# Value products of prompt attention: one head's values in two parts as the stationary operand, two passes and a sum

## The chip, the cores and the metric

One core of one Trainium2 chip runs the whole program. The metric is the device time of one execution in microseconds (us). The profile was taken of a single execution on that core; times of instructions are in us unless ns is written.

## What is computed

One inference step of a layer with two groups of attention heads side by side, then a gated feed-forward part, for 512 prompt tokens and 8 x 16 sampled tokens (640 tokens together, model width 2048). One input projection gives queries, keys and values of group A (16 heads of width 64, a frame sees its own chunk of 64 and the eight before it) and of group B (16 query heads over 2 key and value heads, window of 128, sinks, partial rotary). The core of a head is

```python
p = jnp.exp(s - m)
denom = jnp.sum(p, axis=-1, keepdims=True)
w = (p / denom).astype(v.dtype)
o = jnp.einsum('bghrqk,bgkhd->bgqhrd', w, v)
...
o = jnp.concatenate([rmsnorm(oa, norm_grp_a), rmsnorm(ob, norm_grp_b)], axis=-1)
x = x + o @ w_out
h = rmsnorm(x, norm_ffn)
return x + (jax.nn.silu(h @ w_gate) * (h @ w_up)) @ w_down
```

The change concerns the `einsum` of `w` and `v` for the prompt tokens, in both groups.

## The kernel before, in words

Everything is held with features (or keys) in the 128 partitions and tokens along the free axis. The matmuls take their operands as float32r; to keep float32 accuracy each operand is split into a rounded part `hi` and a rest `lo` (`split`, lines 137 to 139: ACT writes `hi`, DVE subtracts to give `lo`), and each product takes three passes, `hi*hi + hi*lo + lo*hi` (`mm3`, lines 145 to 149). So line 147, 148 and 149 are the first, second and third pass of every product in the program, and lines 138 and 139 are the two halves of every split.

The order of work. `dense` (line 159) computes one 128-row tile of an output for all 640 tokens: for each block of 8 feature tiles it splits the weights (two slots each for `hi` and `lo` and two blocks at a time, so the next block's split can begin when the block before the present one is done with), then issues 6 matmuls of 320 columns for each feature tile. After each of these groups of 6 it calls `pump` (line 72), which emits one more stage of the side work. Side work is attention, written as generators: each `yield` ends a stage. Two streams of heads run beside the projections; from p = 4 on (line 660) one of the two streams is given to the sampled tokens ("decode"), so that the prompt heads of group A have the other alone. The framework then orders the instructions of each engine itself from these emissions, within the dependences; each engine works through its own list in order.

Slots. On-chip tiles are handed out in order of return from lists ("S": 128 x 640 floats, "W": 128 x 1024 floats). `n.bank()` takes one of four PSUM banks ("at") for side work; the projections have two pairs of their own ("dn").

A head of group A (`prompt_a`, line 354): scores of four query tiles with a mask and a maximum on DVE, exponentials on ACT, division on DVE, then `flip` (line 341): transposes of the 128 x 128 blocks into a bank, split into `hi` and `lo`. The value product follows (lines 376 to 384): with `v` of 128 key rows by 128 columns as the stationary operand, `p` moves through in pieces of 512, 384, 128 and 256 columns, three passes each, all into one bank `ps`. The 128 columns of `v` are the values of two heads, 64 each, but a head needs only its own 64 rows of the output; `tensor_copy` (line 387) takes these rows to the tile `ot`. When both heads of a pair are done, `ot` is written to `oa_d` in DRAM, which the output projection reads back much later (line 680).

A head of group B (`prompt_b`, line 390) does the same with pieces of 256, 256, 256 and 128 columns (lines 412 to 416) and the copy of line 419; here the 128 columns of `vb` are the two value heads.

The values themselves are made in `values` (line 448): transposes of the projected tile into a bank, then one split of 128 x 512 into `hi` and `lo`; for group B also the 128 sampled tokens, of which `decode_b` uses `cut(vb, SP, TOK)` (line 506).

Of the kernel before, what the change touches and what calls it, by code (L numbers as in the profile page):

```python
# [13 lines left out]
P = 128  # L14
D = 2048
KT = 16
TOK = 640
# [14 lines left out]


def active(step):
    """Pairs of ff tiles on chip in a step of the second half: each stays for eight steps."""
    return [j for j in range(NPAIR) if (step - START[j]) % STEPS < 8]


# [9 lines left out]


class Net:  # L50
    """Emission helpers over a fixed set of on-chip slots handed out in program order."""

    def __init__(self, nc, tc, io, pools):
        self.nc, self.tc, self.io, self.pools = nc, tc, io, pools
# [15 lines left out]
        self.queues.setdefault(queue, []).append(work)  # L70

    def pump(self):
        """Emit one more stage of the side work; streams take turns."""
        for _ in range(len(self.streams)):
            name, queue = self.streams[self.turn % len(self.streams)]
            self.turn += 1
            work = self.active.get(name)
            if work is None and self.queues.get(queue):
                work = self.active[name] = self.queues[queue].pop(0)
            if work is None or work.gi_running:  # L80
                continue
            try:
                next(work)
            except StopIteration:
                self.active[name] = None
            return True
        return False
# [21 lines left out]
        self.lists.setdefault(lst, []).extend(self.owner.pop(id(t))[0] for t in tiles)  # L109

    def keep_turns(self):
        """A slot's tiles take it in program order."""
        first = {}
        for block in self.nc.cur_f.blocks:
            for ins in block.instructions:
                for o in ins.outs or ():
                    ap = getattr(o, "bass_ap", None)
                    if ap is not None:
                        first.setdefault(ap.tensor.name, ins)
        info = mybir.DependencyInfo(mybir.DependencyClass.NoSync, mybir.DependencyReason.DATA)  # L120
        for names in self.turns.values():
            for x, y in zip(names, names[1:]):
                self.tc.add_manual_dep(first[y], first[x].name, info, reason="slot order")
# [21 lines left out]
    def mm3(self, out, a, b, first, last):  # L145
# [2 lines left out]
        mm(out, a[0], b[1], start=False, stop=False)  # L148
        mm(out, a[1], b[0], start=False, stop=last)  # L149

    def weights(self, src, kt, lst="WH"):
        raw, hi, lo = self.get("WR"), self.get(lst), self.get(lst)
        self.nc.sync.dma_start(out=sh(raw, kt, P), in_=src)
        w = [r(sh(hi, kt, P)), r(sh(lo, kt, P))]
        self.split(sh(raw, kt, P), *w)
        self.put("WR", raw)
        return kt, w, (lst, hi, lo)

    def dense(self, chunks, acts, outs=1):
        """One tile of outputs, or several that share the passes over acts."""  # L160
        ps = [self.banks() for _ in range(outs)]
        k = 0
        for i in range(0, len(chunks), outs):
            now = [c if len(c) == 3 else self.weights(*c) for c in chunks[i:i + outs]]
            for j in range(now[0][0]):
                ah, al = acts[k]
                for (_, w, _), out in zip(now, ps):
                    for a in range(2):
                        t = slice(a * HT, a * HT + HT)
                        self.mm3(out[:, a], (w[0][:, j], w[1][:, j]), (ah[:, t], al[:, t]), k == 0, k == len(acts) - 1)  # L170
                    self.pump()
                k += 1
            for _, _, own in now:
                self.put(*own)
        return ps if outs > 1 else ps[0]

    def rstd_steps(self, parts, dim, out):
        """1 / sqrt(mean + eps) of the tokens of each half, in all partitions."""
        nc = self.nc
        ps, n = self.bank(), len(parts)  # L180
        blocks = (0, P, HT - P)
# [43 lines left out]
def r(ap):  # L225
    return ap.bitcast(F32R)


def build(nc, tc, io, pools):
# [31 lines left out]
    oa_d, ob_d = dram("oa_d", (8, P, TOK)), dram("ob_d", (8, P, TOK))  # L261
    sa_d, sb_d = dram("sa_d", (3, P, 8, P)), dram("sb_d", (P, 8, P))

# [1 line left out]
    n.move("S", "C", 7)  # L265
    n.move("S", "F", 3)
    n.move("W", "WR", 2)
    n.move("W", "WH", 4)
    r_mix, cos, sin, kb0, kb1, vb0, vb1 = (n.get("C") for _ in range(7))
    kb, vb = (r(kb0), r(kb1)), (r(vb0), r(vb1))  # L270

# [1 line left out]
    START_CHUNKS = {0: (24, 0, 2, "S"), 1: (25, 0, 2, "S"), 2: (24, 2, 8, "WH"), 4: (25, 2, 8, "WH"),  # L273
                    8: (24, 8, 16, "W"), 10: (25, 8, 16, "W")}
    xg, acts, xs = [], [], []
# [38 lines left out]
        nc.vector.tensor_tensor(halves(out), ps, halves(r_mix), ALU.mult)  # L314
        return out

# [1 line left out]
    def scores(q, k, rr, i, k0, k1, bias, s, mx):  # L318
        ps = n.bank()[:, :k1 - k0]
        rows = slice(64 * rr, 64 * rr + 64)  # L320
# [33 lines left out]
    def prompt_a(h, q, k, v, ot, done):  # L354
# [19 lines left out]
        o1, p13 = flip([blk(i, 1) for i in range(1, 4)] + [blk(3, 3)], "S")  # L374
        yield
        ps = n.bank()
        n.mm3(ps, cut(v, 0, 128), p0, True, False)
        n.put("S", *o0)
        o2, p2 = flip([blk(i, 2) for i in range(2, 4)], "S")
        n.put("S", t0, t1)  # L380
        yield
        n.mm3(ps[:, 128:], cut(v, 128, 256), cut(p13, 0, 384), False, False)
        n.mm3(ps[:, 384:], cut(v, 384, 512), cut(p13, 384, 512), False, False)
        n.mm3(ps[:, 256:], cut(v, 256, 384), p2, False, True)
        n.put("S", *o1, *o2)
        rows = slice(64 * rr, 64 * rr + 64)
        nc.vector.tensor_copy(ot[rows, :SP], ps[rows])
        done()

    def prompt_b(t, rr, q, ot, done):  # L390
        sink = sinks[:, 8 * rr + t:8 * rr + t + 1]
        t0, t1 = n.get("S"), n.get("S")
        es = [t0[:, 512:640], t0[:, :256], t0[:, 256:512], t1[:, :256]]
        mx = n.small(4)
        for pick in ((0, 1), (2, 3)):
            for i in pick:
                k0 = max(0, i - 1) * P
                w = (i + 1) * P - k0
                scores(q, kb, rr, i, k0, k0 + w, mask_b[:, 256 - w:], es[i], mx[:, i:i + 1])
            yield  # L400
        softmax(es, mx, sink)
        yield
        yield
        yield
        yield
        oa, pa = flip([es[0], es[1][:, :P], es[2][:, P:], es[3][:, :P]], "S")
        yield
        ob, pb = flip([es[1][:, P:], es[2][:, :P], es[3][:, P:]], "S")
        n.put("S", t0, t1)
        yield  # L410
        ps = n.bank()
        n.mm3(ps[:, 0:256], cut(vb, 0, 128), cut(pa, 0, 256), True, False)
        n.mm3(ps[:, 256:512], cut(vb, 256, 384), cut(pa, 256, 512), False, False)
        yield
        n.mm3(ps[:, 128:384], cut(vb, 128, 256), cut(pb, 0, 256), False, False)
        n.mm3(ps[:, 384:512], cut(vb, 384, 512), cut(pb, 256, 384), False, True)
        n.put("S", *oa, *ob)
        rows = slice(64 * rr, 64 * rr + 64)
        nc.vector.tensor_copy(ot[rows, :SP], ps[rows])
        done()  # L420

    def heads_of(kind, p, held, *args):
# [22 lines left out]
        nc.vector.tensor_tensor(x[:80], x[:80], rot[:80], ALU.add)  # L445
        n.put("S", rot)

    def values(vf, hi, lo, cols):
        for c in range(0, cols, 512):
            w = min(512, cols - c)  # L450
            ps = n.bank()[:, :w]
            for j in range(w // P):
                tr(ps[:, j * P:(j + 1) * P], vf[:, c + j * P:c + (j + 1) * P])
            n.split(ps, hi[:, c:c + w], lo[:, c:c + w])

    def decode_b():
        os_b = n.get("W")
        o_s = sh(os_b, 8, P)
        for hf in range(2):
# [17 lines left out]
            for bb in range(4):  # L477
# [25 lines left out]
                yield  # L503
                po = n.bank()[:, :256]
                n.mm3(po, (vd[0][:, bb], vd[1][:, bb]), cut(pt2, 0, 256), True, False)
                n.mm3(po, cut(vb, SP, TOK), cut(pt2, 256, 512), False, True)
                n.put("S", *own)
                for j in range(2):
                    rows = slice(64 * j, 64 * j + 64)
# [95 lines left out]
        dma(out=oa_d[4 * g:4 * g + 4, :, SP:].rearrange("t p c -> p t c"), in_=sh(o_s, 4, P))  # L605
        n.put("D", o_s, bias, *z, *held)

# [1 line left out]
    n.add("heads", input_norm())  # L609
    ps_k, ps_v = n.dense(first, acts, 2)  # L610
    n.drain()
# [4 lines left out]
    n.put("F", kf)  # L616
    vf = proj(25, ps_v)
    dma(out=io["o_vb"], in_=vf)
    values(vf, *vb, TOK)
    n.put("F", vf)  # L620

    def project_b(t):
# [9 lines left out]
    def project_a(p):  # L632
# [16 lines left out]
        dma(out=sa_d[2, :, p], in_=vf[:, SP:])  # L649
        vo = n.get("W")  # L650
        v = pack(vo, SP)
        values(vf, *v, SP)
        n.put("F", vf)
        heads_of(prompt_a, p, [("W", x) for x in (ko, qo, vo)], q, k, v)

# [13 lines left out]
            n.add("decode", decode_a(0))  # L669
        project_a(p)  # L670

# [1 line left out]
    n.put("S", *xg, r_mix)  # L673
    n.move("F", "S", 3)

# [33 lines left out]
    n.put("S", r_b, *own_b)  # L709
    n.move("D", "S", 10)  # L710

# [1 line left out]
    more = group_operands(oa_d, g_a, ssq_a, range(4, 8))  # L713
    own_a, acts_a = own_a + more[0], acts_a + more[1]

    def prepare(kts, in_place=()):
        """The seven left operands of pairs of feature tiles, one product at a time."""
        work = []
        for kt in kts:
            scale = lambda t, m: nc.scalar.activation(t[:, :TOK], x2[m], AF.Identity, scale=g_ffn[:, m:m + 1])  # L720
# [45 lines left out]
                pass  # L766
    n.put("S", r_a, ssq_a, *own_a)

# [1 line left out]
    n.move("WH", "H", 4)  # L770
    n.move("WR", "W1", 2)
    n.lists["W"] = n.lists.pop("W1") + n.lists["W"]

    def quartet(k, load, lefts, before=None, after=None, part="all"):
        """Weights b11, b12, b21, b22 against the seven left operands; yields each
        product's name and bank. The late part has the two products that only add
        to the first half of the tokens."""

        def product(src, which, bank):
            own = n.get("H"), n.get("H")  # L780
# [126 lines left out]
                n.put("S", *gate, *y)  # L907
    n.put("S", r_f)

# [1 line left out]
    sums, waiting = [], []  # L911

    def fetch_waiting(left):
# [59 lines left out]
            for i in range(2):  # L973
                n.add_square(ssq, sums[t % 8][i], t == STEPS - 8 and i == 0, "S")

# [1 line left out]
    r_y = n.get("S")  # L977

    def squares(q, half):
# [129 lines left out]
```

## Time and profile before

| what | value |
|---|---|
| runs of the kernel (us) | 2723.32, 2725.25, 2726.64; median 2725.25 |
| span of the profiled execution, first to last instruction | 2722.2 us |
| its mean granted TensorE clock | 0.988 |
| instructions in the profile | 45156 |
| largest groups of PE | lines 147, 148 and 149, 3694 matmuls of 320 columns each into "dn" |

The page gives the profiled execution no time other than its span, which is 3.05 us below the median of the runs; sums made from its rows are set against 2722.2 us and carried over to 2725.25 us as a difference.

How to read it: a row of a timeline gives the start, the duration, the engine, the line and the operation. PE is TensorE's matmuls, PEld its loads of the stationary operand, which run beside the matmuls. A matmul's duration includes its way through the array and overlaps the next one, so what a matmul costs is the distance from its start to the start of the next. "idle before, releaser" names what an engine last waited for. The granted clock is a share of full speed. Tile names have their numbers left out: "at" is a side-work bank, "dn" a projection bank, "S", "W" and "C" slots.

### The profile page before, as it was taken

Reading aid. Unit: us, or ns where it says so; the run is one execution under the profiler, and the core shown is the slowest. Engines: PE = TensorE matmul, PEld = TensorE weight load, DVE = VectorE, ACT = ScalarE, POOL = GpSimd, SP = SyncE. Lnnn points to the kernel's source line nnn. Section 1 sums busy time; section 2 is a strip of 40 time slices with the busy share of each in tenths; the row PEclk is TensorE's granted clock in tenths of the full one; section 3 lists DMA queues with packets and bytes.
Section 4 is the critical chain, followed back from the end, with each engine's and each line's share of the span. In section 5 each row is a group of like instructions: output and inputs, shape, how many; then the busy total and the mean of one; then the engine's idle time right before and its main releaser. Section 6 shows DMA issues by size and latency. Waiting matters only on the chain.

```text
span 2722.2 us, 45156 instructions
## 1 busy us (share of the span) xinstructions
PE 2645.7 (97%) x17757; PEld 2584.7 (95%) x17757; DVE 1933.8 (71%) x2947; ACT 1063.8 (39%) x1718; POOL 787.2 (29%) x564
## 2 busy tenths in 40 slices
PE   7999999999999999999999999999999899999986
PEld 7999999899899999999999999999999899999986
DVE  6555565655666678776767667667677878888897
ACT  4333333433544454333333333333334444444443
POOL 3000000000212123333343333333434533444453
PEclk9999999999899999999999999999999999999998
DMA  5222223333556443333232333332334644444334
GB/s 163 86 77 76 82 75 100 108 117 113 165 182 214 148 141 109 103 105 124 96 119 103 111 116 106 108 119 101 120 103 152 228 130 130 134 127 133 109 115 134
DMA packets 154149, 332.25 MB, mean 122 GB/s; under 512 B 18065, under 2 KB 69265, under 8 KB 153937
## 3 DMA queue, kind: packets, MB, share of 16 engines
q1 hardware_dynamic: 153936, 329.38, 36.9%
q8 instruction: 139, 2.28, 0.3%
q14 instruction: 74, 0.60, 0.1%
HBM read 274.38 MB, written 54.20 MB: 121 GB/s over the span
## 4 chain that ended last, share of the span: by engine, by line
PE 60%; DVE 5%; DMA 3%; issue 2%; ACT 1%; POOL 1%; SPq 0%; DVEq 0%; POOLq 0%; ACTq 0%
PE dn L149 12%; PE dn L147 12%; PE dn L148 12%; PE at L149 8%; PE at L148 8%; PE at L147 8%; DVE W L139 2%; DMA S<-act_d 1%; DVE S L828 1%; DMA W<-w_down 1%; DVE S L999 0%; DVE S L139 0%; DVE W L809 0%; DVE S L841 0%; POOL S L212 0%
## 5 line engine op out<-in xcount | busy, mean ns | idle before, releaser
L147 PE MATMUL dn<-S,W 128*128 128x320 f32 x3694 | 1164.8, 315 | 16.4 <-DVE S L828 6.3
L149 PE MATMUL dn<-S,W 128*128 128x320 f32 x3694 | 1150.5, 311 | 16.4 <-DVE W L139 16.4
L148 PE MATMUL dn<-S,W 128*128 128x320 f32 x3694 | 1148.9, 311 | 2.2 <-DVE S L143 1.1
L138 ACT ACTIVATE W<-W 128x1024 fp32r<-128x1024 f32 (+2 forms) x632 | 609.4, 965 | 1085.3 <-PE dn L148 551.4
L139 DVE TENSOR_TENSOR W<-W,W 128x1024 fp32r<-128x1024 f32 (+2 forms) x632 | 770.1, 1219 | 134.8 <-ACT W L138 130.2
L147 PEld LDWEIGHTS dn<-S,W 128*128 128x128 f32 x3694 | 699.5, 189 | 35.1 <-issue 17.3
L149 PEld LDWEIGHTS dn<-S,W 128*128 128x128 f32 x3694 | 699.4, 189 | 21.3 <-DVE W L139 21.0
L148 PEld LDWEIGHTS dn<-S,W 128*128 128x128 f32 x3694 | 700.0, 190 | 4.0 <-DVE S L143 1.4
L149 PE MATMUL at<-S,W 128*128 128x320 f32 (+2 forms) x1658 | 514.3, 310 | 7.5 <-DVE W L139 7.4
L147 PE MATMUL at<-S,W 128*128 128x320 f32 (+2 forms) x1658 | 513.6, 310 | 1.1 <-ACT W L138 1.1
L148 PE MATMUL at<-S,W 128*128 128x320 f32 (+2 forms) x1658 | 513.3, 310 | 0.2 <-DVE S L139 0.2
L811 POOL TENSOR_TENSOR W<-W,W 128x1024 f32<-128x1024 f32 (+2 forms) x76 | 162.8, 2142 | 587.0 <-DVE W L139 450.6
L149 PEld LDWEIGHTS at<-S,W 128*128 128x128 f32 x1658 | 311.3, 188 | 11.0 <-DVE W L139 10.3
L147 PEld LDWEIGHTS at<-S,W 128*128 128x128 f32 x1658 | 311.4, 188 | 1.6 <-ACT W L138 1.4
L148 PEld LDWEIGHTS at<-S,W 128*128 128x128 f32 x1658 | 311.3, 188 | 0.5 <-DVE S L139 0.5
L828 DVE TENSOR_TENSOR S<-S,dn 128x320 f32<-128x320 f32 x358 | 164.2, 482 | 104.0 <-PE dn L149 102.7
L807 DVE TENSOR_TENSOR W<-W,W 128x1024 f32<-128x1024 f32 (+2 forms) x76 | 140.2, 1845 | 89.4 <-DMA W<-w_up 46.6
L818 POOL TENSOR_TENSOR W<-W,W 128x1024 f32<-128x1024 f32 (+2 forms) x76 | 166.7, 2193 | 112.5 <-DVE W L139 107.0
L828 DVE TENSOR_TENSOR S<-S,at 128x320 f32<-128x320 f32 x262 | 123.5, 481 | 71.0 <-PE at L149 71.0
L212 POOL TENSOR_TENSOR S<-S,S 128x640 f32<-128x640 f32 x40 | 75.3, 1882 | 161.8 <-ACT S L211 161.4
L809 DVE TENSOR_TENSOR W<-W,W 128x1024 f32<-128x1024 f32 (+2 forms) x76 | 82.9, 1090 | 31.8 <-DMA W<-w_gate 23.0
L139 DVE TENSOR_TENSOR S<-at,S 128x512 fp32r<-128x512 f32 (+2 forms) x108 | 64.0, 604 | 53.0 <-ACT S L138 52.2
(141 smaller groups left out, 2306.6 us busy)
## 6 DMA issues: line engine op xcount, KB each, us to landing
W<-w_gate SPq DMA_DIRECT2D x88, 512.0 KB
W<-w_up SPq DMA_DIRECT2D x88, 512.0 KB
W<-w_in SPq DMA_DIRECT2D x66, 512.0 KB
W<-w_down SPq DMA_DIRECT2D x64, 384.0 KB
W<-w_down SPq DMA_DIRECT2D x68, 320.0 KB
act_d<-S SPq DMA_DIRECT2D x66, 320.0 KB
half<-act_d SPq DMA_DIRECT2D x81, 160.0 KB
S<-act_d SPq DMA_DIRECT2D x80, 160.0 KB
```

The source lines that it names most:

```text
L138: self.nc.scalar.activation(hi, src, AF.Identity)
L139: self.nc.vector.tensor_tensor(lo, src, f(hi), ALU.subtract)
L147: mm(out, a[0], b[0], start=first, stop=False)
L148: mm(out, a[0], b[1], start=False, stop=False)
L149: mm(out, a[1], b[0], start=False, stop=last)
L212: (eng or nc.gpsimd).tensor_tensor(ssq, ssq, sq, ALU.add)
L807: nc.vector.tensor_tensor(b12[:, w], b12[:, w], b22[:, w], sub)
L809: nc.vector.tensor_tensor(s6[:, w], b11[:, w], b12[:, w], sub)
L811: nc.gpsimd.tensor_tensor(b11[:, w], b22[:, w], s6[:, w], sub)
L818: nc.gpsimd.tensor_tensor(b21[:, w], b21[:, w], s6[:, w], sub)
L828: add = lambda o, a, b: nc.vector.tensor_tensor(o, a, b, ALU.add)
```

## The change

A second helper takes two passes with one stationary operand. The tile with one head's values now holds `hi` and `lo` side by side, 64 columns each, for each block of 128 keys, so the passes give `hi*p` in output rows 0 to 63 and `lo*p` in rows 64 to 127, with `p` being `hi` and then `lo` of the weights. A new `both` moves the lower half of the bank by ACT into an "S" slot and adds the upper half to it on DVE. `values` makes one such tile for each of two heads with two splits of half the size; the own values of the sampled tokens in group B get a tile view of their own (`vb_own`). Comments and docstrings are removed too.

```diff
+    def mm2(self, out, a, b, first, last):
+        mm = self.nc.tensor.matmul
+        mm(out, a, b[0], start=first, stop=False)
+        mm(out, a, b[1], start=False, stop=last)
...
-    kb, vb = (r(kb0), r(kb1)), (r(vb0), r(vb1))
+    kb = (r(kb0), r(kb1))
+    vb_own = tuple(r(x[:, SP:]) for x in (vb0, vb1))
...
         ps = n.bank()
-        n.mm3(ps, cut(v, 0, 128), p0, True, False)
+        vr = v[rr]
+        n.mm2(ps, vr[:, 0:128], p0, True, False)
...
-        n.mm3(ps[:, 128:], cut(v, 128, 256), cut(p13, 0, 384), False, False)
-        n.mm3(ps[:, 384:], cut(v, 384, 512), cut(p13, 384, 512), False, False)
-        n.mm3(ps[:, 256:], cut(v, 256, 384), p2, False, True)
+        n.mm2(ps[:, 128:], vr[:, 128:256], cut(p13, 0, 384), False, False)
+        n.mm2(ps[:, 384:], vr[:, 384:512], cut(p13, 384, 512), False, False)
+        n.mm2(ps[:, 256:], vr[:, 256:384], p2, False, True)
         n.put("S", *o1, *o2)
-        rows = slice(64 * rr, 64 * rr + 64)
-        nc.vector.tensor_copy(ot[rows, :SP], ps[rows])
+        both(ot, rr, ps)
         done()
...
-        n.mm3(ps[:, 0:256], cut(vb, 0, 128), cut(pa, 0, 256), True, False)
-        n.mm3(ps[:, 256:512], cut(vb, 256, 384), cut(pa, 256, 512), False, False)
-        yield
-        n.mm3(ps[:, 128:384], cut(vb, 128, 256), cut(pb, 0, 256), False, False)
-        n.mm3(ps[:, 384:512], cut(vb, 384, 512), cut(pb, 256, 384), False, True)
+        vr = r((vb0, vb1)[rr])
+        n.mm2(ps[:, 0:256], vr[:, 0:128], cut(pa, 0, 256), True, False)
+        n.mm2(ps[:, 256:512], vr[:, 256:384], cut(pa, 256, 512), False, False)
+        yield
+        n.mm2(ps[:, 128:384], vr[:, 128:256], cut(pb, 0, 256), False, False)
+        n.mm2(ps[:, 384:512], vr[:, 384:512], cut(pb, 256, 384), False, True)
         n.put("S", *oa, *ob)
-        rows = slice(64 * rr, 64 * rr + 64)
-        nc.vector.tensor_copy(ot[rows, :SP], ps[rows])
+        both(ot, rr, ps)
         done()
...
-    def values(vf, hi, lo, cols):
-        for c in range(0, cols, 512):
-            w = min(512, cols - c)
-            ps = n.bank()[:, :w]
-            for j in range(w // P):
-                tr(ps[:, j * P:(j + 1) * P], vf[:, c + j * P:c + (j + 1) * P])
-            n.split(ps, hi[:, c:c + w], lo[:, c:c + w])
+    def values(vf, sides):
+        ps = n.bank()
+        for j in range(4):
+            tr(ps[:, j * P:(j + 1) * P], vf[:, j * P:(j + 1) * P])
+        for rr, v in enumerate(sides):
+            src = ps.rearrange("p (j c) -> p j c", j=4)[:, :, 64 * rr:64 * rr + 64]
+            v = v.rearrange("p (j c) -> p j c", j=4)
+            n.split(src, v[:, :, :64], v[:, :, 64:])
+
+    def both(ot, rr, ps):
+        t = n.get("S")
+        nc.scalar.activation(t[:64, :SP], ps[64:], AF.Identity)
+        nc.vector.tensor_tensor(ot[64 * rr:64 * rr + 64, :SP], t[:64, :SP], ps[:64], ALU.add)
+        n.put("S", t)
...
-                n.mm3(po, cut(vb, SP, TOK), cut(pt2, 256, 512), False, True)
+                n.mm3(po, vb_own, cut(pt2, 256, 512), False, True)
...
-    values(vf, *vb, TOK)
+    values(vf, [r(x[:, :SP]) for x in (vb0, vb1)])
+    ps = n.bank()[:, :P]
+    tr(ps, vf[:, SP:])
+    n.split(ps, *vb_own)
...
-        values(vf, *v, SP)
+        values(vf, v)
```

## Rows read from the trace of the kernel before

**Rows 1.** The page: span, and busy time of each engine.

```profile
span 2722.2 us, 45156 instructions
...
PE 2645.7 (97%) x17757; PEld 2584.7 (95%) x17757; DVE 1933.8 (71%) x2947; ACT 1063.8 (39%) x1718; POOL 787.2 (29%) x564
```

**Rows 2.** Busy time by stage: stretch, length, PE, PEld, DVE, ACT, POOL (instructions), clock, DMA.

```profile
57.00:440.00 383.00, 382.45 (x2618) 364.71 (x2618) 217.12 (x518) 129.31 (x307) 5.35 (x12) 1.00 0.24 81
440.00:770.00 330.00, 326.65 (x2141) 303.05 (x2140) 212.91 (x549) 144.02 (x324) 33.53 (x82) 0.98 0.38 126
```

**Rows 3.** Timeline, PE, one A head's value product: start, us, engine line operation.

```profile
169.88 0.39 PE L149 MATMUL at<-S,W 128*128 128x512 f32 x1
...
170.11 0.38 PE L248 MATMUL at<-cst,S 128*128 128x128 f32 x2
...
171.56 0.35 PE L149 MATMUL at<-S,W 128*128 128x384 f32 x1
...
171.74 0.22 PE L147 MATMUL at<-S,W 128*128 128x128 f32 x1
...
171.91 0.27 PE L149 MATMUL at<-S,W 128*128 128x128 f32 x1
...
172.03 0.33 PE L147 MATMUL at<-S,W 128*128 128x256 f32 x1
...
172.31 0.28 PE L149 MATMUL at<-S,W 128*128 128x256 f32 x1
...
172.43 0.31 PE L147 MATMUL dn<-S,W 128*128 128x320 f32 x1
```

**Rows 4.** Groups by shape, 57 to 770 us, PE: counts of the third passes.

```profile
L149 PE MATMUL at<-S,S 128*128 128x256 f32 x64 | 18.0, 283 | 0.0
...
L149 PE MATMUL at<-S,W 128*128 128x512 f32 x16 | 6.3, 394 | 0.0
...
L149 PE MATMUL at<-S,S 128*128 128x128 f32 x16 | 4.4, 273 | 0.0
```

**Rows 5.** Groups by shape, 57 to 770 us, ACT and DVE reading a bank, with their waits.

```profile
L139 DVE TENSOR_TENSOR S<-at,S 128x512 fp32r<-128x512 f32 x59 | 40.0, 688 | 39.9 <-ACT S L138 39.5
...
L138 ACT ACTIVATE S<-at 128x512 fp32r<-128x512 f32 x59 | 34.8, 593 | 63.8 <-PE at L248 61.5 <-DMA S<-S 2.1
...
L419 DVE COPY S<-at 64x512 f32<-64x512 f32 x16 | 11.0, 687 | 16.0 <-PE at L149 16.0
...
L387 DVE COPY S<-at 64x512 f32<-64x512 f32 x16 | 11.0, 687 | 3.7 <-PE at L149 3.5
...
L139 DVE TENSOR_TENSOR S<-at,S 128x256 fp32r<-128x256 f32 x16 | 6.7, 420 | 7.1 <-ACT S L138 7.1
...
L138 ACT ACTIVATE S<-at 128x256 fp32r<-128x256 f32 x16 | 6.1, 380 | 19.5 <-PE at L248 10.9 <-DVE S L445 8.6
```

**Rows 6.** Timeline: weight splits on ACT and DVE in a stretch without attention.

```profile
70.97 1.06 ACT L138 ACTIVATE W<-W 128x1024 fp32r<-128x1024 f32 x1 [5.35 <-issue]
...
72.06 1.23 DVE L139 TENSOR_TENSOR W<-W,W 128x1024 fp32r<-128x1024 f32 x1 [0.17 <-ACT W L138]
...
77.96 1.06 ACT L138 ACTIVATE W<-W 128x1024 fp32r<-128x1024 f32 x1 [5.93 <-PE dn L148]
```

**Rows 7.** Line 387's copies by stage: stretch, length, DVE (instructions), clock, DMA share, GB/s.

```profile
440.00:770.00 330.00, 6.85 (x10) 0.98 0.38 126
```

**Rows 8.** Busy time in short stretches, columns as rows 2.

```profile
710.00:715.00 5.00, 4.14 (x30) 3.78 (x29) 3.25 (x7) 4.28 (x6) 3.35 (x6) 1.00 0.60 204
715.00:720.00 5.00, 5.00 (x20) 3.83 (x19) 3.42 (x8) 4.16 (x7) 1.99 (x2) 0.55 0.54 167
720.00:725.00 5.00, 5.00 (x20) 4.56 (x19) 3.91 (x8) 1.12 (x2) 2.70 (x3) 0.50 0.61 204
```

**Rows 9.** Tile oa_d, its writes and reads: durations in ns, first and last start.

```profile
L429 SPq DMA_DIRECT2D oa_d<-S x8: 326/327/327, 175.9 to 768.6; - x8
L680 SPq DMA_DIRECT2D S<-oa_d x8: 320/323/434, 829.5 to 874.6; - x8
```

## Prediction

> **What bounds the kernel now.** I read the page first: TensorE's matmuls are busy in 97% of a span of 2722.2 us, the next engine, DVE, in 71% [rows 1]. A busy share is an average, so the second view is the busy time by stage. The value products of the prompt lie in two stages, from 57 to 440 us (two streams of prompt heads beside the projections) and from 440 to 770 us (one stream of prompt heads, one of sampled tokens). In the first, PE is busy in 382.45 of 383 us at full clock; in the second in 326.65 of 330 us at a mean clock of 0.98 [rows 2]. ACT has 129.31 and 144.02 us of work there, DVE 217.12 and 212.91, and the DMA engines are busy in 24% and 38% [rows 2]. So in both stages the order of PE's own instructions sets the end: a matmul less is time less, unless PE then waits for something it does not wait for now.
>
> Next I read what a matmul costs, from the distance of starts in the timeline, since durations overlap. Then I read how often each shape occurs (groups by shape), what the evictions and splits cost on ACT and DVE (the same view), and how early a weight split is finished before PE needs it (the timeline of ACT and DVE).
>
> **Third passes taken away.** In the value product of a group A head the third pass of 512 columns holds PE for 170.11 - 169.88 = 0.23 us, that of 384 columns for 171.74 - 171.56 = 0.18, that of 128 for 172.03 - 171.91 = 0.12, and that of 256 for 172.43 - 172.31 = 0.12 [rows 3]. Together 0.65 us for a head, and 16 heads give 10.4 us. A group B head has three pieces of 256 columns and one of 128: 3 x 0.12 + 0.12 = 0.48 us, for 16 heads 7.7 us. The counts agree: 16 third passes of 512 columns for A; 64 of 256 columns from S tiles, of which 48 are B's and 16 the sampled tokens', which stay; 16 of 128 columns for B [rows 4]. The stationary loads that go with them run beside matmuls and are already inside these distances. Removed: 128 matmuls, 18.1 us of PE. The two passes that remain are of the same shape as before (128 rows, 128 stationary columns), so I leave their price as it is.
>
> The Trainium skill (TensorE: Matmul & The Clock Gate, Back-to-back issue gap) puts an isolated matmul at its columns over 2.4 GHz plus 2.5 ns. My estimate from that page would be 14.8 us for the 128 passes, since it gives 0.056 us to 128 columns, where the row has 0.12; the time would be 2710.5 by it. The measured distance decides.
>
> **The new eviction.** Before, DVE copied 64 x 512 from the bank in 0.687 us [rows 5]. Now ACT first moves 64 x 512, then DVE adds 64 x 512. Neither shape is in the trace; the nearest rows are an ACT move of 128 x 512 out of a bank, 0.593 us, and a DVE operation of 128 x 512 with one input in a bank and one in a slot, 0.688 us [rows 5]. So DVE's work stays as it is (0.687 against 0.688), and ACT gets 32 x 0.593 = 19.0 us more. ACT's 273.3 us of work in 713 us [rows 2] become 292, so the time is there; the question is only what waits behind it. I take 0. The bounds: none of it seen by PE, 0; all of it, 19.0 us, which would eat the gain. No gain is to be had from it. I lean to the lower end because of the waits of the copies now. DVE, which also makes the second half of every weight split in order, already stands still before line 419 for 16.0 us over 16 copies and before line 387 for 3.5 [rows 5], and PE still loses only 0.55 of 383 us. ACT would stand still in the same places.
>
> **What is queued behind ACT's wait.** ACT now waits at this point for the last value matmul, and behind it stand exponentials and splits, of the next weight block too. In a stretch without attention the block's `hi` begins at 70.97 us, its `lo` begins at 72.06 and takes 1.23, so it is ready at 73.29; PE gets through to the next block at about 77.96, where ACT can begin the next split [rows 6]. That is a slack of 4.7 us, against a mean wait of 1.0 us for a copy of line 419 (16.0 over 16) plus 0.6 of work. The splits are covered by it. With the cover gone, each late block would cost up to 1.06 + 1.23 = 2.29 us.
>
> **The bank and the slot.** The bank goes back some 0.6 us later for each head, the duration of ACT's move. There are four side banks; a stage that finds none would make PE wait. Bounds: 0 and again 19.0 us; I take 0, since PE's idle time in the first stage is 0.55 us in all [rows 2], so bank returns are not what it waits for. The slot of `both` is taken right after the flips' slots came back, so the list is never empty there, and it is returned at once; later tiles move on by one slot. That can shift a load by a wait of this size, either way, by amounts that I can't price beyond the 3.35 us that PE idles in the second stage [rows 2]. For the last head of A all this is free: the last write of `oa_d` is issued by 768.6 us and the first read begins at 829.5 [rows 9].
>
> **The values.** One split of 128 x 512 becomes two of 128 x 256 with gaps between runs of 64: ACT 2 x 0.380 - 0.593 = +0.17 us, DVE 2 x 0.420 - 0.688 = +0.15 us [rows 5], eight times for A and once for B: 1.5 us on ACT and 1.4 on DVE, beside PE. What the gaps cost is not in the trace; even double the price of these eighteen splits would lie beside PE, for the heads begin some stages later. I take 0, with 1.4 us as the upper bound, should each DVE part be waited for. Transposes stay 4 for a tile (5 for B's).
>
> **The sum.** 18.1 us less, against the profiled span: 2722.2 - 18.1 = 2704.1. The median of the runs is 3.05 us above that span, and I carry the difference over: 2725.25 - 18.1 = 2707.15, so 2707 us.
>
> **Rivals.** First, **slower by ACT's order**. ACT works through its list in order, so an eviction that waits for PE at the end of a weight block holds up that block's successor, and PE then stands for 2.29 us. The Trainium skill (TensorE: Matmul & The Clock Gate, the table at its head) calls the queues of ScalarE and VectorE strict first-in first-out, eight deep; the timeline's in-order waits agree. With half of the heads hit: 16 x 2.29 = 36.6, so 2725.25 - 18.1 + 36.6 = 2744. It decides from 18.1 / 2.29, eight heads, on. For it: the wait is new on ACT. Against it: the slack of 4.7 us, and DVE's waits that cost nothing. Chance 0.07.
>
> Second, **part of the gain is lost in the second stage**. Ten of A's copies lie in it [rows 7], so 10 x 0.65 = 6.5 us of the saving. Around 700 to 750 us PE already waits for the sampled tokens' chain: busy 4.14 of 5 us from 710 to 715 [rows 8]. If all ten savings end in such waits, 11.6 us remain: 2713.7. A second stretch at half clock of the kind in the third rival would give about the same, 2713.8. Against it: PE is busy in 326.65 of 330 us there. Chance 0.15.
>
> Third, **the clock**. After the wait at 710 to 715 us, the granted clock is 0.55 and 0.50 for the next ten us [rows 8], the lower of its two levels (1.2 of 2.4 GHz). A mean of 0.98 over 330 us is 6.6 us of lost time [rows 2]. If the new order of instructions closes that gap, 2700.6; if it opens another alike, the second rival's time. Chance of the gain 0.10.
>
> Fourth, **it does not do what it says**: the saved passes are given back where a stage is paced by something else, such as the loads of weights. Then it stays at 2725. The DMA engines' 24% and 38% [rows 2] speak against. Chance 0.08.
>
> **How the numbers follow.** The forecast itself, 18.1 us with a few us either way, has 0.60. I count as no difference what is within 0.2%, 5.45 us, about what a measurement of this kernel can tell: 2719.8 to 2730.7. Faster are the forecast, the second and the third rival: 0.60 + 0.15 + 0.10 = 0.85; the same, 0.08; slower, 0.07. The range goes from 2698, the third rival with 2 to 3 us of luck, to 2718, the second with some 4 us of the bounds for banks, slot and values. It leaves out the fourth and the first, 0.15.
>
> **What would show it.** Right: 128 matmuls fewer, none on the third-pass line between value tiles of the prompt; PE as busy as before in both stages and the end of the attention stages about 11 us earlier at the old 440 mark (six A heads at 0.65 and B's 7.7 make 11.6) and 18 earlier at the old 770; the ACT move at about 0.6 us, the add at about 0.69. Wrong: waits of PE for line 138 or 139 on W tiles or for a bank, in the order of microseconds; an ACT move over 1 us; a longer stretch at 0.5 clock after 700 us; or an equal saving that later stages give back.

## The result, and the profile after

The changed kernel took 2707.55 us (median of 4 runs, 2703.80 to 2711.32) against 2724.78 us for the kernel before (4 runs in all). The ratio is 0.9945, with a 95% interval of 0.9932 to 0.9958. The same kernel measured once more gave 0.9951 [0.9939, 0.9964]. So it is faster by 13 to 17 us: by 15.0 (ratio) or 17.2 (medians) on the first occasion, by 13.3 or 12.7 on the second. The profiled execution has a span of 2705.0 us, 17.3 less than before (2704.95 against 2722.22).

The page's busy times answer to [rows 1], and the stages to [rows 2], with the same columns.

```profile
span 2705.0 us, 44972 instructions
...
PE 2629.3 (97%) x17629; PEld 2568.5 (95%) x17629; DVE 1928.6 (71%) x2956; ACT 1084.0 (40%) x1759; POOL 786.9 (29%) x564
```

```profile
57.00:440.00 383.00, 382.12 (x2590) 363.11 (x2589) 221.92 (x534) 145.22 (x338) 4.96 (x12) 1.00 0.26 84
440.00:770.00 330.00, 324.26 (x2147) 301.45 (x2146) 219.00 (x567) 154.90 (x345) 36.70 (x88) 0.99 0.43 134
```

There are 17757 - 17629 = 128 matmuls less, and PE's busy time fell by 16.4 us. ACT has 20 us more work, and the span is shorter by about what PE's work lost. PE is nearly as full as before: it stands idle for 0.88 us of the first stage, where it was 0.55, and for 5.74 us of the second, where it was 3.35.

Next comes the timeline of one A head's last three value pieces, which answers to [rows 3] (line 154 is the first pass of the new helper, 155 the second).

```profile
169.36 0.34 PE L154 MATMUL at<-S,W 128*128 128x384 f32 x1
169.53 0.34 PE L155 MATMUL at<-S,W 128*128 128x384 f32 x1
169.71 0.22 PE L154 MATMUL at<-S,W 128*128 128x128 f32 x1
169.77 0.27 PE L155 MATMUL at<-S,W 128*128 128x128 f32 x1
169.88 0.33 PE L154 MATMUL at<-S,W 128*128 128x256 f32 x1
170.05 0.28 PE L155 MATMUL at<-S,W 128*128 128x256 f32 x1
170.17 0.31 PE L147 MATMUL dn<-S,W 128*128 128x320 f32 x1
```

The passes that remain cost what they did: 0.18 us for 384 columns, 0.11 to 0.12 for the others' second pass. Summed over the trace, from the start of each of the prompt's value passes to the next start on PE, the value products took 53.4 us before and 36.0 after: 17.4 us less.

The last view is the groups by shape from 50 to 760 us, with the waits of the new eviction (468 is ACT's move, 469 DVE's sum), answering to [rows 4, 5]; below it, what line 468 waited for and who waited for it (the source's own view), and the longest of its waits (the waits of ACT: total, times, longest).

```profile
L469 DVE TENSOR_TENSOR S<-S,at 64x512 f32<-64x512 f32 x32 | 21.7, 679 | 17.2 <-ACT S L468 16.9
L468 ACT ACTIVATE S<-at 64x512 f32<-64x512 f32 x32 | 19.0, 596 | 28.4 <-PE at L155 28.2
...
L155 PE MATMUL at<-S,S 128*128 128x256 f32 x48 | 12.7, 283 | 0.0
L155 PE MATMUL at<-S,W 128*128 128x512 f32 x16 | 6.3, 394 | 0.0
...
L155 PE MATMUL at<-S,S 128*128 128x128 f32 x16 | 4.5, 280 | 0.0
```

```profile
  PE at L155: 28.2, 20
who waited for it (us, times):
  DVE S L469: 16.9, 16
  ACT W L138: 6.2, 2
  PEld at L147: 0.6, 3
```

```profile
ACT S L468 <- PE at L155: 28.2, 20, 3.5
```

ACT stands still for value products 28.2 us in 20 waits, the longest 3.5 us, and of all that 0.6 us reaches PE's loads. The 6.2 us before ACT's weight splits (W, line 138) are not the move's doing: the longer of the two waits, 5.95 us, ended 5.9 us after the move that the view names was done, so something else ended it; the other is 0.2 us.

### The profile page after: what moved, and what is told of

Same layout as the page of the kernel before. It is cut to its first block, busy times and chain, and to the rows that moved or that the text cites. A ratio compares the mean times of both kernels' runs of the same rounds, so it can differ in the third digit from the quotient of the medians.

```text
span 2705.0 us, 44972 instructions
## 1 busy us (share of the span) xinstructions
PE 2629.3 (97%) x17629; PEld 2568.5 (95%) x17629; DVE 1928.6 (71%) x2956; ACT 1084.0 (40%) x1759; POOL 786.9 (29%) x564
## 4 chain that ended last, share of the span: by engine, by line
PE 84%; DVE 8%; DMA 4%; issue 3%; ACT 2%; SPq 0%; DVEq 0%; POOL 0%; ACTq 0%
PE dn L147 18%; PE dn L149 17%; PE dn L148 17%; PE at L147 9%; PE at L149 9%; PE at L148 9%; DVE W L139 2%; PE at L254 1%; DVE S L847 1%; DMA S<-act_d 1%; DMA W<-w_down 1%; DVE S L139 1%; PE at L155 1%; PE at L154 1%; DVE S L1018 0%
## 5 line engine op out<-in xcount | busy, mean ns | idle before, releaser
L147 PEld LDWEIGHTS dn<-S,W 128*128 128x128 f32 x3694 | 700.6, 190 | 33.2 <-issue 16.9
L149 PE MATMUL at<-S,W 128*128 128x320 f32 x1594 | 494.4, 310 | 7.0 <-DVE W L139 6.6
L147 PE MATMUL at<-S,W 128*128 128x320 f32 x1594 | 493.5, 310 | 1.5 <-ACT W L138 1.5
L148 PE MATMUL at<-S,W 128*128 128x320 f32 x1594 | 493.0, 309 | 0.0
L149 PEld LDWEIGHTS at<-S,W 128*128 128x128 f32 x1594 | 299.5, 188 | 10.2 <-DVE W L139 10.2
L147 PEld LDWEIGHTS at<-S,W 128*128 128x128 f32 x1594 | 299.9, 188 | 1.7 <-ACT W L138 1.7
L148 PEld LDWEIGHTS at<-S,W 128*128 128x128 f32 x1594 | 299.6, 188 | 0.0
L826 DVE TENSOR_TENSOR W<-W,W 128x1024 f32<-128x1024 f32 (+2 forms) x76 | 134.5, 1770 | 103.9 <-DMA W<-w_up 52.4
L828 DVE TENSOR_TENSOR W<-W,W 128x1024 f32<-128x1024 f32 (+2 forms) x76 | 82.9, 1091 | 30.7 <-DMA W<-w_gate 24.1
```

The source lines that it names most:

```text
L147: mm(out, a[0], b[0], start=first, stop=False)
L826: nc.vector.tensor_tensor(b12[:, w], b12[:, w], b22[:, w], sub)
L828: nc.vector.tensor_tensor(s6[:, w], b11[:, w], b12[:, w], sub)
```

## Experiments

All ratios are to the kernel before, on the same chip in the same stretch of time; the interval of each is about 0.0013 either way unless given. The first three take the change apart.

**A third pass put back.**

```diff
         mm(out, a, b[0], start=first, stop=False)
-        mm(out, a, b[1], start=False, stop=last)
+        mm(out, a, b[1], start=False, stop=False)
+        mm(out, a, b[1], start=False, stop=last)
```

> The changed kernel with a third pass put back (the second one issued twice, so the product of the lo weights counts double); layout, eviction by ACT and DVE and split stay as changed. Theory (the gain is the 128 passes on PE): +18.0 us on the changed kernel, so 2725, level with the kernel before; 128 matmuls more. Rival (the gain comes from the new layout, eviction or order of instructions): it stays near 2708. Rival (eviction and splits cost PE time which the passes outweigh): it ends above the kernel before, by that cost, 2727 to 2744.

Measured: 0.9993 [0.9984, 1.0002], no difference from the kernel before. Its page has PE's old work:

```profile
PE 2645.3 (97%) x17757; PEld 2585.8 (95%) x17757; DVE 1936.5 (71%) x2956; ACT 1081.5 (40%) x1759; POOL 786.5 (29%) x564
```

Everything of the change but the missing pass is in this kernel, and the gain is gone. So the passes carry the gain; layout, eviction, splits and slots together cost nothing by themselves that can be measured (by the interval they cost at most 0.5 us, and give at most 4.4).

**Group A alone, and group B alone** (the other group's layout, passes and copy as before the change).

> Group A's value products in two passes, group B's as before the change. Theory: 16 x 0.65 = 10.4 us less than before, 2714.4. Rival (what is saved beside the sampled tokens' chain is lost in waits): only the six heads of the first stage count, 3.9 us less, 2720.9.

> Group B's value products in two passes, group A's as before the change. Theory: 16 x 0.48 = 7.7 us less than before, 2717.1; the parts of A and B add up to the whole. Rival (the ends of two B heads fall together, so that two evictions stand on ACT before the next head's splits, 0.6 us late for each of 8 pairs): 4.8 us given back, 2721.9.

Measured: 0.9960 [0.9946, 0.9973] and 0.9957 [0.9945, 0.9970], 11 and 12 us. To see where, I take the starts of DVE's reads of finished projection tiles (the same tiles in each kernel) as landmarks in the profiled executions, and list how much earlier (minus) or later (plus) each comes than in the kernel before:

| landmark, at (us before) | 88.2 | 442.5 | 713.0 | 764.2 | 910.6 | end, 2722.2 |
|---|---|---|---|---|---|---|
| third pass put back | +0.4 | +0.6 | +0.6 | -2.6 | -2.9 | -3.6 |
| A alone | -1.7 | -5.4 | -9.8 | -13.1 | -9.7 | -15.2 |
| B alone | +1.0 | -4.9 | -5.0 | -8.5 | -8.7 | -13.7 |
| the change | -1.2 | -10.6 | -13.7 | -17.3 | -16.8 | -17.3 |
| the change, measured again | -0.9 | -10.4 | -15.1 | -18.2 | -17.8 | -18.7 |

From 88 to 442 us A alone gains 3.7 (six heads at 0.65 make 3.9), B alone 5.9 (7.7 forecast), both 9.4. B alone and the change each lose 1.7 us there in a stretch at the lower clock (shown further down); without it they gain 7.6 and 11.1. From 442 to 713 us, beside the sampled tokens, A alone gains 4.4 where eight heads at 0.65 make 5.2; the change gains 3.1 in its first profile and 4.7 in its second. So the rival that this part is lost there falls, but for a remainder of 0.5 to 2 us.

From 713 to 764 us every kernel of the table gains 3.1 to 3.6 us, also the one with all its passes. That is no saving of the passes: the execution profiled before has its half-clock stretches there [rows 8], and the others have less of them. So single profiles can't be added up across that stage.

The measured parts, 11 and 12 us, come to more than the whole, 13 to 15, and B's part to more than its 7.7. A good part of that is the clock: the five runs of B alone had a mean granted clock of 0.9896, those of the kernel before beside them 0.9885, while the changed kernel on its second occasion had 0.9876 against 0.9888. My estimate, the difference of the clocks times 2722 us, takes 0.7 us from A's part, 2.9 from B's and adds 3.2 to the 13.3 of the whole: 10.2 and 8.8 against 16.5. With an interval of 3.5 us either way on each, no difference from the forecast's 10.4, 7.7 and 18.1 is left that the runs could tell.

**The sum left out**, to see what the eviction costs: DVE copies the upper half alone, and the lo part of the values is not added. It was measured twice, the second time beside the changed kernel.

```diff
-        t = n.get("S")
-        nc.scalar.activation(t[:64, :SP], ps[64:], AF.Identity)
-        nc.vector.tensor_tensor(ot[64 * rr:64 * rr + 64, :SP], t[:64, :SP], ps[:64], ALU.add)
-        n.put("S", t)
+        nc.vector.tensor_copy(ot[64 * rr:64 * rr + 64, :SP], ps[:64])
```

> The changed kernel without the sum: DVE copies the upper half of the bank, the lo part of the values is left out, ACT moves nothing. Theory (eviction hidden beside PE): within 2 us of the changed kernel, 2705.5 to 2709.5, while ACT loses 19 us of work. Rival (ACT's new wait in its order costs PE time): faster by what it costs, the 2 to 3 us by which the stage with the heads gained less than 18.1, so 2704 to 2706, or more.

> The changed kernel itself once more, beside the next one on the same chip. Theory (128 passes, 18 us of PE): a ratio to the kernel before of 0.9935. The first measurement gave 0.9945 [0.9932, 0.9958]; if it stays near 0.9945, some 3 us of the passes' worth are given back each time.

> The changed kernel without the sum once more (DVE copies the upper half, the lo part of the values is left out). Theory (eviction hidden): level with the changed kernel of this call within 0.1%. Rival (the eviction costs the 2.5 us that the two ratios so far differ by, 0.9935 against 0.9945): again faster by 0.1% or more.

Measured: 0.9935 and 0.9936 without the sum, 0.9945 and 0.9951 with it.

**ACT's move four times**, and **the move on DVE**:

```diff
-        nc.scalar.activation(t[:64, :SP], ps[64:], AF.Identity)
+        for _ in range(4):
+            nc.scalar.activation(t[:64, :SP], ps[64:], AF.Identity)
...
+        nc.vector.tensor_copy(t[:64, :SP], ps[64:])
```

> The changed kernel with ACT's move of the lower half made four times instead of once: 96 moves more, 57 us of ACT work, and 1.8 us more hold of ACT and of the bank for each head. Theory (slack of some 4.7 us before a weight split is needed): within 3 us of the changed kernel, 2705 to 2711. Rival (ACT's strict order reaches PE): a good part of 57 us shows, 2720 or more.

> The changed kernel with the move of the lower half on DVE, so ACT has no part in the eviction and DVE 22 us more. Theory (hidden on either engine): within 2 us of the changed kernel. Rival (ACT's new wait costs): 2 to 3 us faster. Rival (DVE is the nearer bound, about 60% busy there): slower by 2 us or more.

Measured: 0.9947 with four moves, 0.9932 with the move on DVE. The first page shows the added work, and the view of the line who waited for it (with the loop the move is line 469 and the sum 470):

```profile
PE 2629.8 (97%) x17629; PEld 2568.1 (95%) x17629; DVE 1929.0 (71%) x2956; ACT 1132.2 (42%) x1855; POOL 784.6 (29%) x564
```

```profile
L469 ACT ACTIVATE S<-at x128: 577/595/600, 96.8 to 756.6; 64x512 f32<-64x512 f32 x128
...
who waited for it (us, times):
  DVE S L470: 27.6, 16
  PEld at L147: 0.2, 1
```

By the ratio, 128 moves instead of 32 on ACT cost nothing that can be measured, and PE's loads wait 0.2 us for the moves themselves. But what stands behind the moves on ACT does come late. In the timeline of the same kernel the transposes of one A head were done at 167.6 us (line 254), the split of their bank (line 138) began behind two moves that had waited for the other head's value product, and PE waited for it:

```profile
167.20 0.38 PE L254 MATMUL at<-cst,S 128*128 128x128 f32 x2
...
169.31 1.23 ACT L469 ACTIVATE S<-at 64x512 f32<-64x512 f32 x2 [2.87 <-PE at L155]
...
170.56 0.38 ACT L138 ACTIVATE S<-at 128x256 fp32r<-128x256 f32 x1
...
171.00 0.38 PE L154 MATMUL at<-S,W 128*128 128x256 f32 x1 [0.32 <-ACT S L138]
```

This happens three times in the first stage, at 0.32 us each. So ACT's strict order (rival one) reaches PE with four moves, but by 0.3 us now and then, not by 2.29 us for a head; the changed kernel has no such wait in that stage.

Yet the three measurements with the move on ACT (0.9945, 0.9951, 0.9947; mean 0.9948) all lie above the three without it (0.9935, 0.9936, 0.9932; mean 0.9934). Each pair's intervals overlap; the means differ by 0.0013, some 3.6 us, and in the two pairs that ran side by side (changed kernel and no sum, four moves and DVE's move) the medians differ by 3.1 and 3.8. The mean granted clocks of these pairs don't explain it (0.9876 and 0.9876, 0.9886 and 0.9882). Nor do the profiles show it: at the landmark of 764.2 us, behind nearly all of the evictions, the two profiles of the changed kernel are 17.3 and 18.2 us ahead of the kernel before, and those without the move on ACT 16.9, 18.5 (no sum) and 16.9 (move on DVE). Only the profile with four moves lags there, 13.3 ahead. And the kernel with the third pass put back has the same eviction and stands level with the kernel before. So whether the move costs these 3.6 us, and by what, was not settled.

**One pass alone** (the lo part of the weights is left out):

```diff
-        mm(out, a, b[0], start=first, stop=False)
-        mm(out, a, b[1], start=False, stop=last)
+        mm(out, a, b[0], start=first, stop=last)
```

> The changed kernel with one pass alone in the value products (the lo part of the weights is left out). Theory (PE's list sets the end, pass by pass): the second passes are worth 16 x 0.64 + 16 x 0.47 = 17.8 us, so 2689.7. Rival (another engine's chain takes over after the first saving, in the second stage above all): less than half of that, 2699 or more.

Measured: 0.9865 [0.9850, 0.9880], 0.0083 below the changed kernel's mean of 0.9948 (23 us, with an interval of 3.5 either way on each of the two). The next 128 passes are worth at least as much as the first; no other engine's chain takes over. The changed kernel lies 12 us below the one with the third pass put back and 23 above this one, where the distances of starts promise 17.4 and 17.8: as if some 5 us were missing in the changed kernel alone, hardly more than these intervals allow.

**Scores in two passes too.** The scores are products over 64 rows (one head's width). In the changed kernel's timeline, one of them in group A:

```profile
147.20 0.31 PE L149 MATMUL dn<-S,W 128*128 128x320 f32 x1
147.44 0.32 PE L147 MATMUL at<-W,W 64*128 64x128 f32 x1
...
147.82 0.44 PE L147 MATMUL at<-W,W 64*128 64x512 f32 x1
148.10 0.39 PE L148 MATMUL at<-W,W 64*128 64x512 f32 x1
148.33 0.39 PE L149 MATMUL at<-W,W 64*128 64x512 f32 x1
148.66 0.42 PE L147 MATMUL dn<-S,W 128*128 128x320 f32 x1
148.91 0.31 PE L148 MATMUL dn<-S,W 128*128 128x320 f32 x1
```

The first pass takes 0.28 us and the last 0.33 up to the next start, against 0.23 for the middle one and for 128 rows [rows 3]. The projection's matmuls of 320 columns beside the group are dearer too: 0.24 us just before it and 0.25 just behind it. First group B alone is stacked: queries hi over lo in 128 rows, keys hi twice and then lo twice.

```diff
+        for rr in range(2):
+            rows, other = slice(64 * rr, 64 * rr + 64), slice(64 - 64 * rr, 128 - 64 * rr)
+            nc.scalar.activation(qb[rr][rows], qf[rows, :SP], AF.Identity)
+            nc.vector.tensor_tensor(qb[rr][other], qf[rows, :SP], f(qb[rr])[rows], ALU.subtract)
...
-                scores(q, kb, rr, i, k0, k0 + w, mask_b[:, 256 - w:], es[i], mx[:, i:i + 1])
+                n.mm2(ps, q[rr][:, 128 * i:128 * i + 128],
+                      (k_hi[rr][:, k0:k0 + w], k_lo[rr][:, k0:k0 + w]), True, True)
```

> The changed kernel, and group B's scores in two passes too: a head's queries hi and lo stand one above the other in 128 rows, against keys hi and then lo, both doubled over the rows. The result is the same but that lo*lo is added. Theory (PE's list sets the end): 48 passes of 256 columns and 16 of 128 less, 16 x 0.47 = 7.5 us, and what a product over 64 rows costs more than one over 128 (0.05 us in the first pass, up to 0.08 behind the third) in part, so 2693 to 2700. Rival (the splits of queries and keys, twice as many on ACT and DVE, come late for the scores, or two slots less hold up the heads): 2705 or more.

Measured: 0.9883 [0.9869, 0.9896], 2692.18 us, just below the 2693 to 2700 that the theory expected. Then group A as well, at first with a second pass over 64 rows to save slots:

```diff
-        n.mm3(ps, (q[0][rows, qs], q[1][rows, qs]), (k[0][rows, ks], k[1][rows, ks]), True, True)
+        nc.tensor.matmul(ps, q[rr][:, qs], k[rr][:, ks], start=True, stop=False)
+        nc.tensor.matmul(ps, q[rr][rows, qs], k[2][rows, ks], start=False, stop=True)
```

> Scores of both groups in two passes: group B as in the run that stacked B alone; group A with a head's queries hi over lo against keys hi doubled over the rows (128 rows), then queries hi against keys lo (64 rows). Theory (PE's list sets the end): 16 third passes of 512, 384, 256 and 128 columns less, 16 x 0.65 = 10.4 us, so 10 to 14 us below the 0.9883 of the run that stacked B alone: 0.983 to 0.985. Rival (one more S slot for each pair of heads, and five half-height operations more for each pair on ACT and DVE, hold the heads up beside the sampled tokens): 0.987 or more.

Measured: 0.9904 [0.9890, 0.9917]: nothing gained over group B alone, as the rival said, but not for the rival's reason. The timeline shows the same product (329 over 128 rows, 330 over 64):

```profile
146.42 0.51 PE L329 MATMUL at<-W,W 128*128 128x512 f32 x1
146.86 0.49 PE L330 MATMUL at<-S,W 64*128 64x512 f32 x1
147.28 0.42 PE L147 MATMUL dn<-S,W 128*128 128x320 f32 x1
```

Two passes take 0.86 us, where three took 0.84: 0.44 and 0.42 instead of 0.23. Summed over the trace, from start to start and without waits, the score products of group A take 42.0 us here, 37.3 with group B alone stacked. So two passes of unequal height cost more than three of equal height. PE's waits are not the reason: between the landmarks at 442.5 and 764.2 us it stands idle for 5.9 us in both kernels. The last kernel gives the second pass 128 rows too (keys lo doubled, in one more slot for each pair):

```diff
-        nc.tensor.matmul(ps, q[rr][rows, qs], k[2][rows, ks], start=False, stop=True)
+        nc.tensor.matmul(ps, q[rr][:, qs], k[2 + rr][:, ks], start=False, stop=True)
```

> As the run that stacked the scores of both groups, but group A's second pass also over 128 rows (keys lo doubled over the rows, in a second S slot for each pair). Theory (in that run each change between passes of 128 and of 64 rows cost about 0.2 us, 0.435 us from a 128-row pass of 512 columns to the next start against 0.231 among equals, which ate the third pass's worth): without the changes A's scores take 16 x 1.23 = 20 us instead of some 37 to 39, so 17 us below the run that stacked B alone, a ratio near 0.982. Rival (the fewer S slots and the added half-height splits held the heads up, and would more so now): 0.988 or more.

Measured: 0.9842 [0.9828, 0.9855], 2680.4 us. The same product there:

```profile
144.75 0.31 PE L149 MATMUL dn<-S,W 128*128 128x320 f32 x1
144.90 0.22 PE L328 MATMUL at<-W,W 128*128 128x128 f32 x1
...
145.07 0.45 PE L328 MATMUL at<-W,W 128*128 128x512 f32 x1
145.35 0.40 PE L329 MATMUL at<-S,W 128*128 128x512 f32 x1
145.59 0.30 PE L147 MATMUL dn<-S,W 128*128 128x320 f32 x1
145.73 0.31 PE L148 MATMUL dn<-S,W 128*128 128x320 f32 x1
```

0.52 us for it instead of 0.84, and 20.9 us for group A's score products in all. The projection's matmuls before and behind the group are back at 0.15 and 0.14 us. The first pass still takes 0.28, so the 0.05 that it has over the others is not the height's. This version is 43 us faster than the kernel before and about 28 faster than the changed one. It stays some 6 us short of the 0.982 expected; in its profile PE stands idle for 9.2 us between the landmarks at 442.5 and 764.2 us, instead of 5.1 and 3.9 in the two of the changed kernel and 5.9 with group B alone stacked, so the rival about the held-up heads may have a part of it; no run shows that apart.

## Why the prediction was right, and where not

Forecast 2707, measured 2707.55; forecast 18.1 us less, measured 17.2 by the medians, 17.3 between the profiles, 15.0 by the ratio, 13.3 by the ratio on the second occasion. Point by point:

- **What bounds it.** PE's list set the end, as read from [rows 2]: a pass put back costs the whole gain, and a pass more taken away gives at least as much again.
- **Third passes.** 18.1 us forecast, 17.4 found between starts. Right to 4%.
- **Durations of the eviction and splits.** ACT's move 0.596 us (0.593 taken), DVE's sum 0.679 (0.688); one of the two splits of half the size 0.386 us on ACT and 0.420 on DVE (0.380 and 0.420). Right.
- **What waits behind ACT.** The slack of 4.7 us was set against a mean wait of 1.0 us; 28.2 us over 32 moves is 0.9, the longest wait 3.5, still under the slack. PE waited for the late half of a weight split once in these stages, 0.8 us, as it did before the change (0.7). The Trainium skill (TensorE: Matmul & The Clock Gate, its first table) gives ScalarE a strict first-in first-out queue. The trace with four moves agrees: a split whose input was there at 167.6 us began at 170.56, behind two moves. What the prediction did not have is that PE pays for splits of attention tiles before it pays for weight splits: 0.32 us, three times, with four moves. Rival one fell.
- **The eviction taken at 0: open.** By six measurements the kernels with the move on ACT end some 3.6 us later than those without it; by the third pass put back, layout and eviction together cost at most 0.5 us. The bounds (0 to 19) hold either. No place where 3.6 us go is seen in the profiles. One that was looked at: in the changed kernel's first pair of B heads DVE comes late with the second half of the queries' split (after the two sums and a weight split), PE waits 0.53 us and then 0.22, and at 103.9 us the clock falls to the lower of its two levels:

```profile
101.31 0.50 PE L149 MATMUL at<-S,S 64*128 64x128 f32 x4 [0.53 <-DVE S L139]
...
104.18 0.47 PE L148 MATMUL dn<-S,W 128*128 128x320 f32 x1
104.44 0.47 PE L149 MATMUL dn<-S,W 128*128 128x320 f32 x1
```

```profile
100.00:105.00 5.00, 4.25 (x29) 3.30 (x26) 4.19 (x20) 0.14 (x1) 0.00 (x0) 0.89 0.46 157
105.00:110.00 5.00, 5.00 (x28) 5.00 (x28) 1.42 (x6) 4.09 (x18) 0.00 (x0) 0.77 0.00 0
```

  The distance of the projection's matmuls goes from 0.147 to 0.266 us. 5 x 0.11 + 5 x 0.23 makes 1.7 us, which is what the projections took longer between the landmarks at 88 and 442 us (1.6). Both profiles of the changed kernel have this stretch, and so has that of B alone; those of the kernel before, of the two without the sum, of the one with the third pass and of the one with four moves have none. But the one with the move on DVE has a longer one (0.93 and 0.50 in the same two stretches) and is no slower, so it does not explain the difference by itself.
- **Rival two** (lost beside the sampled tokens): 4.4 of 5.2 us arrived with A alone, 3.1 and 4.7 with the change. Fell, but for a remainder.
- **Rival three** (the clock): the half-clock stretches between 700 and 750 us were worth some 3 us less in every kernel of the table than in the execution profiled before, passes or not; with the new one at 104 us the sum of both is small: between the landmarks at 88.2 and 764.2 us the clock was at half for 13.7 us in the kernel before and for 10.2 in the changed one, so 1.7 of the 17.3 us gained at the latter are clock. It moved single profiles, not the verdict.
- **Rival four** (no gain): fell.

So the mechanism was right, passes taken from an engine that sets the end, and the landing at half a microsecond from the forecast is partly luck: the ratios give 2 to 4 us less than the passes' 17.4, and the runs of one kernel are spread over 7 us.

## What to carry to other kernels

Where a product uses half of the stationary operand's columns, put the two parts of a split operand side by side there: a third of the passes goes, and the sum of the halves costs little if PE is the bound and the other engines have slack (here at most some 3.6 of 17 us). Where it uses half of the rows, stack the parts there, but give all passes the same height. Price a removed matmul by the distance of starts, not its duration (0.12 us, not 0.28), and judge a change of a few us by a kernel that differs in that one thing, since a single profile moves by 3 us through the clock alone.

## What was not expected of the hardware

A change between a matmul over 128 rows and one over 64 rows costs on both sides, some 0.09 us in the matmul before it and 0.11 in the one behind it. In the changed kernel the projection's 320 columns take 0.239 us from start to start just before a score product of group A and 0.252 just behind one (28 cases each); with the same product over 128 rows, in the last kernel, they take 0.147 and 0.146 in the same places. When heights alternate, each pass pays on both sides: 0.44 and 0.42 us for 512 columns, where 0.23 + 0.09 + 0.11 makes 0.43.

And the granted clock fell to its lower level at 103.9 us, when PE had waited no longer than 0.53 and 0.22 us shortly before. These waits alone don't settle it. With the move on DVE, waits of 0.24 and 0.29 us at 101.3 and 103.1 us were followed by a longer stretch at the lower level; without the sum (second profile), waits of 0.27 and 0.35 us at 101.6 and 102.7 us were followed by none:

```profile
100.00:105.00 5.00, 4.38 (x34) 3.59 (x34) 4.55 (x17) 0.73 (x2) 0.00 (x0) 1.00 0.51 179
105.00:110.00 5.00, 5.00 (x35) 5.00 (x36) 2.31 (x13) 4.24 (x19) 0.00 (x0) 1.00 0.01 4
```

What sets the difference was not tested.
